# FFN down products as seven block products of 2x2 blocks, their sums into x by transfers and VectorE

## The chip, the cores and the metric

One core of a Trainium2 chip runs the kernel. The metric is the device time of one execution in microseconds. TensorE (PE) multiplies, VectorE (DVE) and ScalarE (ACT) do the elementwise work, GpSimd (POOL) and SyncE (SP) issue transfers.

## What is computed

Two layers of an encoder for 640 tokens (512 of a prompt, 8 x 16 of running streams), model width 1024. Each layer is a feed-forward half step, a mixer (convolution and attention branches) and a second feed-forward half step. All is fp32. The part that is changed is the feed-forward:

```python
def _swiglu(h, w_gu, w_down):
    gu = h @ w_gu
    g, u = jnp.split(gu, 2, axis=-1)
    return (jax.nn.silu(g) * u) @ w_down
...
    xp = xp + 0.5 * _swiglu(_rmsnorm(xp, norm_ffn1[l]), w_ffn1_gu[l], w_ffn1_down[l])
```

The inner width is 2816, so 22 inner tiles of 128 rows; the output has 8 tiles of 128.

## The kernel before

Activations lie transposed: `x[m]` is a tile of 128 channels x 640 tokens. fp32 products are made from fp32r parts: each weight and each activation is split into a high part (a ScalarE cast, `whi`, `ahi`) and a low part (a VectorE subtraction, `wlo`, `alo`), and a product is three matmuls: high x high, high x low (activation), low x high (weight). One matmul takes 128 x 128 weights and 320 tokens, half of the 640.

Weights come as a stream of 512 KB transfers (`raw`, three buffers, SP's queue). `prep` makes a slab of 8 weight tiles, 128x1024 (cast L264, low part L269), three buffers each. `slab`, `quiet`, `begin`, `ahead` and `flush` hand out slabs and place the preparation of later ones in the order.

The gate and up products (`gate_up`, a "gu" step, one for each inner tile j) are already made in seven products: the 2x2 block matrix [up; gate] x [even, odd input tiles] times [even, odd input tiles] x [first, second 320 tokens] takes seven block products instead of eight. Three of the seven use sums of weights, which `source` makes with four VectorE additions of 128x512 (L208) on each pair of `raw` tiles, so that 16 weight tiles give 3.5 slabs; `X11, X21, XN6, XT5, XT7, X22, XT4` name the seven forms of the input. A "gu" step is 7 blocks of 12 matmuls. Its accumulators `pa`, `pb`, `pc` are PSUM banks of the tag "att" (four), and ScalarE copies intermediate values of `pa` and `pc` out (`c1` L780, `u2` L791, `c5` L793), since `pa` goes on accumulating. Behind it stands its tail: silu, the product with `rho` (L811), with u (L812), and the split into `ahi` and `alo` (L181, L182).

The 22 inner tiles go in chunks, given by `FFNS`: a0 has (4, 2, 4, 4, 4, 4), b0 (2, 4, 4, 4, 8), a1 (2, 4, 4, 4, 4, 4), b1 (2, 4, 4, 4, 5, 3); a and b are the first and second feed-forward of layers 0 and 1. `ffn_order` puts the down products of one chunk between the gate/up steps of the next, two output tiles after each; those of the last chunk stand at the end. A down product (`product`, L337) of one output tile takes 4 inner tiles x 3 x 2 halves = 24 matmuls into one of two double banks (tag "acc": `pda`, `pdb`), and VectorE adds half of it to `x[m]` (L857, 128x640).

The order on PE, VectorE and ScalarE within a feed-forward is the order in which the program writes the instructions (`manual_schedule`); in the mixer a scheduler orders them. PE's next instruction waits for slabs, for tails and for accumulators that were copied out.

Of the kernel before, what the change touches and what calls it, by code (L numbers as in the profile page):

```python
# [16 lines left out]
P = 128  # L17
D = 1024
L = 2
# [27 lines left out]

PARTS = slice(0, 3 * P), slice(3 * P, T)

XT4, XN6, XT7, X21, X22, X11, XT5 = range(7)  # L50
UW = 2 + SEQ + NB * USEG

# [5 lines left out]
NSM = O_ST + L * CT * NB * 2  # L58


def ffn_order(name):

    chunks, plain = FFNS[name]
    out, held, j0 = [], [], 0
    for n in chunks:
        ms = list(range(KT)) if held else []
        step = max(2, -(-KT // n))
        for j in range(j0, j0 + n):
            out.append(("std" if j < plain else "gu", j))
            if ms:  # L70
                out.append(("down", [(m, held) for m in ms[:step]]))
                ms = ms[step:]
        held = list(range(j0, j0 + n))
        j0 += n

    return out + [("cut", None)] + [("down", [(m, held)]) for m in range(KT)]
# [18 lines left out]
def kinds():  # L95


    out = []

    def plain(n):  # L100
        out.extend([8] * (n // 8) + [n % 8] * (n % 8 > 0))

    def ffn(name):
        held = 0
        for what, a in ffn_order(name):
            if what == "gu":
                plain(held)
                held = 0
                out.append("gu")
            elif what == "std":  # L110
                held += 2 * KT
            elif what == "cut":
                plain(held)
                held = 0
            else:
                held += sum(len(js) for _, js in a)
        plain(held)

    for l in range(L):
        ffn(f"a{l}")  # L120
        held = 0
        for what, _ in mixer_order():
            if what == "mix":
                plain(held)
                held = 0
                out.append("mix")
            else:
                held += {"v": KT * AW // P, "o": KT}.get(what, CT)
        plain(held)
        ffn(f"b{l}")  # L130
    return out
# [11 lines left out]
def trunk(ctx: ExitStack, tc: tile.TileContext, xin, wst, small, pbias, samplebias, kcache, vcache,  # L143
# [36 lines left out]
    def split(hi, lo, src):  # L180
        ACT.copy(hi, src)  # L181
        DVE.tensor_tensor(out=lo, in0=src, in1=hi.bitcast(F32), op=ALU.subtract)  # L182
# [84 lines left out]
    def flush():  # L267
        for lo, src, hi in pending:
            DVE.tensor_tensor(out=lo, in0=src, in1=hi.bitcast(F32), op=ALU.subtract)  # L269
        pending.clear()  # L270
# [20 lines left out]
    def begin():  # L291

        prep(used[0] + 2)
# [30 lines left out]
    def soon():  # L324
        return tc.high_priority(offset=300)

    def steps(ps, ops, at=()):


        n = len(ops)  # L330
        for k, (xh, xl) in enumerate(ops):
            if k in at:
                at[k]()
            wh, wl = tiles.take()
            for j, (w, x) in enumerate(((wh, xh), (wh, xl), (wl, xh))):
                for a in range(2):
                    PE.matmul(ps[:, a, :HT], w, x[:, a * HT : (a + 1) * HT],  # L337
                              start=k == 0 and j == 0, stop=k == n - 1 and j == 2)
            yield

    def product(ps, ops, at=()):
# [362 lines left out]
        with soon():  # L704
            last(pa)

    def gate_up(fp, n, ex, first, turned, tails, put, j):

        pa, pb, pc = (att(f"p{i}{n}")[:, :HT] for i in "abc")

        def cap(name):
            return fp.tile([P, HT], F32, tag="cap", name=f"{name}{n}", bufs=4)

        def mul(ps, s, half, x, ks, start, stop):
            block(ps, s, half, lambda kp: tuple(z[:, x] for z in ex.ops[kp]), ks, start, stop)

        every, most, end = range(NP), range(NP - 1), range(NP - 1, NP)
        g, u = tmp(f"g{n}"), tmp(f"u{n}")
        t1, t2 = slice(0, HT), slice(HT, T)
        c1, u2, c5 = (cap(f"{i}_") for i in ("c1", "u2", "c5"))  # L720
        rho = ex.rho
        if first:

# [53 lines left out]
        else:  # L777
            s0 = quiet()
            mul(pa, s0, 0, X11, every, True, True)
            ACT.copy(c1, pa)  # L780
            prep(used[0] + 1)
            for t in tails:
                t()
            tails.clear()
            flush()
            mul(pb, s0, 1, X21, every, True, True)
            add(u[:, t1], pb, c1)
# [1 line left out]
            flush()  # L789
            mul(pa, s1, 0, XN6, every, False, True)  # L790
            ACT.copy(u2, pa)  # L791
            mul(pc, s1, 1, XT5, every, True, True)
            ACT.copy(c5, pc)  # L793
            s2 = slab(True)[0]
            mul(pa, s2, 0, XT7, every, False, True)
            add(g[:, t2], pa, c5)
            DVE.tensor_tensor(out=g[:, t2], in0=g[:, t2], in1=rho[:, t2], op=ALU.mult)
# [6 lines left out]
        mul(pa, s3, 0, XT4, every, False, True)  # L804
        DVE.tensor_tensor(out=g[:, t1], in0=pa, in1=rho[:, t1], op=ALU.mult)
        ACT.activation(g, g, AF.Silu, scale=-1.0)
        flush()

        def tail():
            begin()  # L810
            DVE.tensor_tensor(out=g, in0=g, in1=rho, op=ALU.mult)  # L811
            DVE.tensor_tensor(out=u, in0=u, in1=g, op=ALU.mult)  # L812
            flush()
            hi = hp.tile([P, T], F32R, tag="hhi", name=f"ahi{n}")
            lo = hp.tile([P, T], F32R, tag="hlo", name=f"alo{n}")
            split(hi, lo, u)
            put(j, (hi, lo))
            ahead()

        tails.append(tail)  # L820
        if first and turned:
            tails.append(ex.inverse)

    def ffn(name, fp, ex, goff, after, end=False):


        act, tails = {}, []
        nxt = None
        chunks, plain = FFNS[name]
        last = FT - chunks[-1]  # L830
        hold[0] = True
        if plain:
            ex = opening(fp, name, goff, plain, act.__setitem__, tails)
        for what, a in ffn_order(name):
            if what in ("std", "cut"):
                continue
            if what == "gu":
                turned = after is not None and not end
                gate_up(fp, f"{name}_{a}", ex, a == plain, turned, tails, act.__setitem__, a)
                continue  # L840
            js = a[0][1]
            if js[0] == last or len(a) * len(js) >= KT:
                for t in tails:
                    t()
                tails.clear()
            if after is not None and js[0] == last:
                nxt = nxt or after()
            if end and js[0] == last:
                nxt.all([act[j] for j in js])
                break  # L850
            for m, js in a:
                pd = acc(f"pd{name}_{js[0]}_{m}")
                product(pd, [act[j] for j in js])
                done = nxt and m == KT - 1
                if nxt:
                    nxt.weights(m)
                DVE.scalar_tensor_tensor(out=halves(x[m]), in0=two(pd), scalar=0.5,  # L857
                                         in1=halves(x[m]), op0=ALU.mult, op1=ALU.add)
                if not done:
                    flush()  # L860
                if nxt:
                    nxt.final(m)
        hold[0] = False
        if not nxt:
            flush()
        return nxt

    def mixer(l, after):
# [633 lines left out]
    for l in range(L):  # L1502
        if l == 0:
            open_pool("fp")
            ex = None
        with tc.manual_schedule(engines=ORDERED):
            ffn(f"a{l}", pool[0], ex, O_G1, None)
        fp.close()

        def after(st):  # L1510
            open_pool(f"fp{l}")
            return Expand(pool[0], f"b{l}", O_G2 + l * KT, st)

        ex = mixer(l, after)
        with tc.manual_schedule(engines=ORDERED):
            if l < L - 1:
                ex = ffn(f"b{l}", pool[0], ex, 0,
                         lambda: Expand(pool[0], f"a{l + 1}", O_G1 + (l + 1) * KT, ex))
            else:
                ffn(f"b{l}", pool[0], ex, 0, Final, True)  # L1520
    fp.close()
    ps.close()

# [7 lines left out]
def _stream(i):  # L1531
# [9 lines left out]
    for l in range(L):  # L1541
        def ffn(name, gu, down):
            g, u = _cols(gu[:, :FF]), _cols(gu[:, FF:])
            d = _cols(down)
            parts, held = [], []
            for what, a in ffn_order(name):
                if what == "gu":
                    if held:
                        parts.append(chunks(held))
                    held = []  # L1550

                    parts.append(chunks([z[a][o::2] for z in (u, g) for o in range(2)]))
                elif what == "std":
                    held += [g[a], u[a]]
                elif what == "cut":
                    parts.append(chunks(held))
                    held = []
                else:
                    held += [d[m][js[0] : js[-1] + 1] for m, js in a]
            return np.concatenate(parts + [chunks(held)])  # L1560
# [88 lines left out]
```

## Time and profile before

| | |
|---|---|
| median of 3 runs | 2574.33 us (2574.31 to 2575.58) |
| profiled execution | 2574.47 us |
| its span, first to last instruction | 2572.7 us |
| PE, VectorE, ScalarE, POOL busy | 99%, 75%, 44%, 2% |
| granted TensorE clock | 0.999 |
| matmuls | 17576 |
| weight stream | 384 transfers of 512 KB, 3.5 us to landing |

The profile's page gives the busy share of each engine, the chain of work that ended last, and groups of instructions by code line with the idle time in front of them. Views of the trace give the same by stretch (windows), in order of time (timeline) and by who waited for whom. `a` and `b` at the end of a tile's name stand for the two feed-forwards of a layer.

### The profile page before, as it was taken

The page shows a single profiled execution, that of the slowest core. Times are in us where ns is not written, and L with a number is a line of the kernel's source. Part 1 is how long each engine was busy: PE and PEld are TensorE (multiplying, and loading weights), DVE is VectorE, ACT ScalarE, POOL GpSimd, SP SyncE. Part 2 cuts the span into 40 slices and gives each one's busy share as a digit, 9 for nine tenths or more (in the row PEclk, how much of TensorE's full clock was granted, in tenths as well). Part 3 has the DMA queues.
Part 4 walks back from the last instruction along what each step waited for, and adds up shares of the span by engine and source line. Part 5 has one row for each costly group of instructions (what it writes and reads, how often), then busy time and mean ns, then how long its engine had stood idle before and what let it go on. Part 6 is the DMA issues. An engine that isn't in the chain of part 4 may idle for free.

```text
span 2572.7 us, 42534 instructions
## 1 busy us (share of the span) xinstructions
PE 2553.6 (99%) x17576; PEld 2497.1 (97%) x17576; DVE 1934.1 (75%) x2973; ACT 1144.7 (44%) x1802; POOL 60.5 (2%) x153
## 2 busy tenths in 40 slices
PE   8999999999999999999999999999999999999998
PEld 8999999888999999999999999998889999999998
DVE  7786767778777987677787767787786778777676
ACT  5343335575444543334444333356644445433333
POOL 0000000111000000000000000001110000000000
PEclk9999999999999999999999999999999999999999
DMA  3222223235222232222222222233442222222222
GB/s 133 66 100 91 81 75 108 99 116 168 75 83 88 74 102 74 81 89 78 83 82 99 74 90 83 74 101 113 134 136 83 74 91 81 92 83 74 91 91 74
DMA packets 74066, 237.05 MB, mean 92 GB/s; under 512 B 8241, under 2 KB 19121, under 8 KB 73873
## 3 DMA queue, kind: packets, MB, share of 16 engines
q1 hardware_dynamic: 70272, 223.90, 26.0%
q0 software_dynamic: 2880, 9.79, 1.1%
q8 instruction: 138, 2.26, 0.4%
q10 hardware_dynamic: 720, 0.65, 0.1%
q14 instruction: 56, 0.45, 0.1%
HBM read 225.85 MB, written 7.94 MB: 91 GB/s over the span
## 4 chain that ended last, share of the span: by engine, by line
PE 92%; DVE 4%; ACT 3%; issue 1%; DMA 0%; ACTq 0%; DVEq 0%
PE pab L351 12%; PE pda L337 12%; PE pdb L337 11%; PE paa L351 11%; PE pcb L351 6%; PE pca L351 5%; PE py L337 4%; PE po L337 4%; PE qa L351 4%; PE pbb L351 3%; PE pba L351 3%; PE pv L1160 2%; PE ma_cv L351 2%; PE ma_qk L351 2%; PE qc L351 2%; PE ma_b L351 1%
## 5 line engine op out<-in xcount | busy, mean ns | idle before, releaser
L269 DVE TENSOR_TENSOR wlo<-raw,whi 128x1024 fp32r<-128x1024 f32 (+2 forms) x540 | 562.5, 1047 | 189.5 <-ACT whi L264 187.3
L264 ACT CAST whi<-raw 128x1024 fp32r<-128x1024 f32 (+2 forms) x540 | 489.9, 912 | 253.7 <-PE pca L351 79.4
L351 PE MATMUL pab<-xhib,whi 128*128 128x320 f32 x704 | 218.4, 310 | 0.4 <-ACT u_b L791 0.4
L351 PE MATMUL pab<-xlob,whi 128*128 128x320 f32 x704 | 217.5, 309 | 0.0
L351 PE MATMUL pab<-xhib,wlo 128*128 128x320 f32 x704 | 217.5, 309 | 0.0
L351 PE MATMUL paa<-xhia,whi 128*128 128x320 f32 x640 | 198.2, 310 | 0.7 <-ACT c_a L727 0.5
L351 PE MATMUL paa<-xloa,whi 128*128 128x320 f32 x640 | 197.7, 309 | 0.0
L351 PE MATMUL paa<-xhia,wlo 128*128 128x320 f32 x640 | 197.7, 309 | 0.0
L337 PE MATMUL pda<-ahia,whi 128*128 128x320 f32 x704 | 160.3, 309 | 0.6 <-DVE x L857 0.6
L337 PE MATMUL pda<-ahia,wlo 128*128 128x320 f32 x704 | 160.4, 309 | 0.0
L337 PE MATMUL pda<-aloa,whi 128*128 128x320 f32 x704 | 160.4, 309 | 0.0
L264 ACT CAST whi<-s 128x1024 fp32r<-128x1024 f32 (+1 forms) x120 | 109.5, 912 | 111.8 <-DVE s L208 85.4
L337 PE MATMUL pdb<-ahib,wlo 128*128 128x320 f32 x656 | 149.5, 309 | 0.0
L337 PE MATMUL pdb<-alob,whi 128*128 128x320 f32 x656 | 149.4, 309 | 0.0
L337 PE MATMUL pdb<-ahib,whi 128*128 128x320 f32 x656 | 149.3, 309 | 0.0
L269 DVE TENSOR_TENSOR wlo<-s,whi 128x1024 fp32r<-128x1024 f32 (+1 forms) x120 | 127.2, 1060 | 13.1 <-ACT whi L264 13.1
L351 PEld LDWEIGHTS pab<-xhib,whi 128*128 128x128 f32 x704 | 132.2, 188 | 1.2 <-ACT u_b L791 0.9
L351 PEld LDWEIGHTS pab<-xlob,whi 128*128 128x128 f32 x704 | 132.2, 188 | 0.2
L351 PEld LDWEIGHTS pab<-xhib,wlo 128*128 128x128 f32 x704 | 132.1, 188 | 0.0
L351 PEld LDWEIGHTS paa<-xhia,whi 128*128 128x128 f32 x640 | 120.1, 188 | 1.3 <-ACT c_a L727 0.8
L351 PEld LDWEIGHTS paa<-xloa,whi 128*128 128x128 f32 x640 | 120.1, 188 | 0.1
L351 PEld LDWEIGHTS paa<-xhia,wlo 128*128 128x128 f32 x640 | 120.1, 188 | 0.0
(582 smaller groups left out, 6952.7 us busy)
## 6 DMA issues: line engine op xcount, KB each, us to landing
raw<-in_wst SPq DMA_DIRECT2D x384, 512.0 KB, 3.5
kc<-in_kcache SPq DMA_DIRECT2D x32, 256.0 KB, 4.0
vc<-in_vcache SPq DMA_DIRECT2D x16, 512.0 KB, 4.5
bias<-in_pbias POOLq DMA_DIRECT2D x16, 256.0 KB, 3.2
x<-in_xin SPq DMA_DIRECT2D x8, 320.0 KB, 5.1
out_vo<-v POOLq DMA_DIRECT2D x10, 256.0 KB, 2.5
out_ko<-k POOLq DMA_DIRECT2D x8, 320.0 KB, 2.5
out_yout<-x SPq DMA_DIRECT2D x8, 192.0 KB, 1.9
```

The lines of the kernel that those rows point to most:

```text
L264: ACT.copy(hi[:, d], src[:, c])
L269: DVE.tensor_tensor(out=lo, in0=src, in1=hi.bitcast(F32), op=ALU.subtract)
L337: PE.matmul(ps[:, a, :HT], w, x[:, a * HT : (a + 1) * HT], start=k == 0 and j == 0, stop=k == n - 1 and j == 2)
L351: PE.matmul(ps, a, b, start=start and kp == 0 and j == 0, stop=stop and kp == NP - 1 and j == 2, skip_group_check=True)
L1160: PE.matmul(pv[t], xx[:, t * P : (t + 1) * P], w[:, kk * AW : (kk + 1) * AW], start=c == 0 and kk == 0 and j == 0, stop=c == KT // 2 - 1 a ...
```

## The change

The down products of a chunk of four inner tiles that is neither the first plain one nor the last (`by_seven`) are made in the same seven-product form: 2x2 blocks of two output tiles by two inner tiles, times two inner tiles by two halves of the tokens. There are 13 such chunks: three in a0, b0 and b1, four in a1.

- A "rows" step (`down_rows`) makes four of the eight output tiles; two of them stand behind the second and the third gate/up step of the next chunk (`ROWS`). It takes 16 weight tiles, prepared as a "gu" slab group, and 7 x 12 = 84 matmuls. It uses both "acc" tiles (A, B) and two "att" banks (c).
- Each pair of inner tiles (`Pair`) gets its seven forms: the tail makes the halves and E1; `rest` makes XN6, XT4, XT7 with their high and low parts in five pieces, and `TURNS` says at which places of the later steps these pieces stand.
- The sums: B, c and the last state of A are added to x by VectorE (`take`, 128x320 each). Four intermediate states (c1, u2, c7 of A, c5 of c) are staged in SBUF by ScalarE with their factor and added to x by accumulating transfers that POOL issues (`send`, two of 128x320 each). The staging tiles are five of 128x2x320 (before: four of 128x320).
- From the third gate/up step of the first such chunk to the end of the gate/up steps only PE keeps the written order; VectorE and ScalarE are ordered by the scheduler.
- In a0 and a1, where the last chunk has four inner tiles, the first two of the final output tiles are multiplied together: for the first three inner tiles of both, then for the fourth of both.

```diff
+TURNS = (
+    ("r0d1", "g3e1", "g3e2", "g3e2", "g3e2"), ("g0e3", "g1e2", "g1e3", "g1e3", "g1e3"),
+    ("g2e3", "g2e4", "g2e7", "g2e7", "g2e7"), ("g0e3", "g0e4", "g0e7", "g0e7", "g0e7"),
+)
+ROWS = (1, 2)
...
-            if ms:
+            if ms and by_seven(name, held[0]):
+                if j - j0 in ROWS:
+                    out.append(("rows", (ms[:4], held)))
+                    ms = ms[4:]
+            elif ms:
...
+        def product(self, n, u, g, hi, lo):
+            if self.E is None:
+                z = self.E = self.fp.tile([P, 3, HT], F32, name=f"de{n}", tag="even", bufs=1)
+                DVE.tensor_tensor(out=z[:, 0:3:2], in0=halves(u), in1=halves(g), op=ALU.mult)
+                DVE.tensor_tensor(out=z[:, 1], in0=z[:, 0], in1=z[:, 2], op=ALU.subtract)
+                at, kinds = slice(0, 2), (X11, XT5)
+            else:
+                z = self.O = self.fp.tile([P, 5, HT], F32, name=f"do{n}", tag="odd", bufs=1)
+                DVE.tensor_tensor(out=z[:, 3:5], in0=halves(u), in1=halves(g), op=ALU.mult)
+                at, kinds = slice(3, 5), (X21, X22)
...
+            flush()
+            ACT.copy(halves(hi), z[:, at])
+            self.low(halves(lo), halves(hi), z[:, at])
...
+        def rest(self):
+            E, O = self.E, self.O
+            for o, a, b in ((XN6, E[:, 1], O[:, 4]), (XT4, O[:, XN6], O[:, 3])):
+                DVE.scalar_tensor_tensor(out=O[:, o], in0=a, scalar=-1.0, in1=b,
+                                         op0=ALU.mult, op1=ALU.subtract)
+            DVE.tensor_tensor(out=O[:, XT7], in0=O[:, 4], in1=E[:, 2], op=ALU.subtract)
+            yield
...
+    def down_rows(fp, n, ms, pairs, tails, later):
...
+        def stage(name, ps, scale=0.5):
+            z = fp.tile([P, 2, HT], F32, tag="cap", name=f"{name}{n}", bufs=5)
+            if ps is A:
+                ACT.activation(z, two(A), AF.Copy, scale=scale)
+            else:
+                for u in range(2):
+                    ACT.activation(z[:, u], ps[u], AF.Copy, scale=scale)
+            return z
+        def send(z, r, cols):
+            for u in range(2):
+                POOL.dma_start(x[ms[2 * u + r]][:, cols], z[:, u], accum_op=ALU.add)
+        def take(ps, r, cols, scale=0.5):
+            for u in range(2):
+                xs = x[ms[2 * u + r]][:, cols]
+                DVE.scalar_tensor_tensor(out=xs, in0=ps[u], scalar=scale, in1=xs, op0=ALU.mult, op1=ALU.add)
+        s0 = quiet()
+        mul(a, s0, 0, X11, True)
+        c1 = stage("c1_", A)
+        prep(used[0] + 1)
+        begin()
+        if not second:
+            tail()
+        flush()
+        place("d1")
+        mul(b, s0, 1, X21, True)
+        take(b, 0, t1)
+        send(c1, 0, t1)
+        s1 = slab(True)[0]
+        flush()
+        mul(a, s1, 0, XN6, False)
+        u2 = stage("u2_", A)
+        mul(c, s1, 1, XT5, True)
+        c5 = stage("c5_", c, -0.5)
+        s2 = slab(True)[0]
+        if second:
+            tail()
+        mul(a, s2, 0, XT7, False)
+        send(stage("c7_", A, -0.5), 1, t2)
+        send(c5, 1, t2)
+        flush()
+        ahead()
+        mul(c, s2, 1, X22, False)
+        take(c, 0, t2)
+        send(u2, 0, t2)
+        s3 = slab(True)[0]
+        ahead()
+        mul(a, s3, 0, XT4, False)
+        take(a, 1, t1, -0.5)
+        flush()
...
+            if what == "gu" and a == free:
+                order({mybir.EngineType.PE})
+            if what == "cut":
+                order(ORDERED)
...
+                    if m == 0:
+                        two_pd = [acc(f"pd{name}_{js[0]}_{i}") for i in range(2)]
+                        ws = [[tiles.take() for _ in js] for i in range(2)]
+                        for ks in (js[:-1], js[-1:]):
+                            for p, w in zip(two_pd, ws):
+                                for j in ks:
+                                    multiply(p, w[j - js[0]], act[j], j == js[0], j == js[-1])
```

More of the change, by code (lines that the diff above doesn't have):

```diff
@@ L58, with chunk_at, by_seven @@
 NSM = O_ST + L * CT * NB * 2
+def chunk_at(name, j):
+    at = 0
+    for n in FFNS[name][0]:
+        if j < at + n:
+            return at, n
+        at += n
+def by_seven(name, j):
+    at, n = chunk_at(name, j)
+    return n == 4 and at >= FFNS[name][1] and at + n < FT
 def ffn_order(name):
@@ L114, in ffn @@
                 held = 0
+            elif what == "rows":
+                plain(held)
+                held = 0
+                out.append("gu")
             else:
@@ L325, in soon, with multiply @@
         return tc.high_priority(offset=300)
+    def multiply(ps, ws, xs, first, last):
+        (wh, wl), (xh, xl) = ws, xs
+        for j, (w, x) in enumerate(((wh, xh), (wh, xl), (wl, xh))):
+            for a in range(2):
+                PE.matmul(ps[:, a, :HT], w, x[:, a * HT : (a + 1) * HT],
+                          start=first and j == 0, stop=last and j == 2)
     def steps(ps, ops, at=()):
@@ L333, in steps @@
                 at[k]()
[L334 to L338, printed above, removed]
+            multiply(ps, tiles.take(), (xh, xl), k == 0, k == n - 1)
             yield
@@ L705, in seven, with gate_up, spot @@
             last(pa)
-    def gate_up(fp, n, ex, first, turned, tails, put, j):
+    def gate_up(fp, n, ex, first, turned, tails, put, j, pair, later, at):
         pa, pb, pc = (att(f"p{i}{n}")[:, :HT] for i in "abc")
         def cap(name):
-            return fp.tile([P, HT], F32, tag="cap", name=f"{name}{n}", bufs=4)
+            return fp.tile([P, 2, HT], F32, tag="cap", name=f"{name}{n}", bufs=5)
         def mul(ps, s, half, x, ks, start, stop):
             block(ps, s, half, lambda kp: tuple(z[:, x] for z in ex.ops[kp]), ks, start, stop)
+        def spot(name):
+            step(later, f"g{at}{name}")
         every, most, end = range(NP), range(NP - 1), range(NP - 1, NP)
@@ L719, in gate_up @@
         t1, t2 = slice(0, HT), slice(HT, T)
-        c1, u2, c5 = (cap(f"{i}_") for i in ("c1", "u2", "c5"))
+        both = cap("c1_")
+        c1, u2, c5 = both[:, 0], both[:, 1], cap("c5_")[:, 0]
         rho = ex.rho
@@ L781, in gate_up @@
             prep(used[0] + 1)
+            spot("e1")
             for t in tails:
@@ L784, in gate_up @@
             tails.clear()
+            spot("e2")
             flush()
@@ L791, in gate_up @@
             ACT.copy(u2, pa)
+            spot("e3")
             mul(pc, s1, 1, XT5, every, True, True)
@@ L794, in gate_up @@
             s2 = slab(True)[0]
+            spot("e4")
             mul(pa, s2, 0, XT7, every, False, True)
@@ L806, in gate_up, with tail @@
         ACT.activation(g, g, AF.Silu, scale=-1.0)
+        spot("e7")
         flush()
-        def tail():
-            begin()
+        def tail(weights=True):
+            if weights:
+                begin()
             DVE.tensor_tensor(out=g, in0=g, in1=rho, op=ALU.mult)
-            DVE.tensor_tensor(out=u, in0=u, in1=g, op=ALU.mult)
-            flush()
             hi = hp.tile([P, T], F32R, tag="hhi", name=f"ahi{n}")
             lo = hp.tile([P, T], F32R, tag="hlo", name=f"alo{n}")
-            split(hi, lo, u)
+            if pair:
+                pair.product(n, u, g, hi, lo)
+            else:
+                DVE.tensor_tensor(out=u, in0=u, in1=g, op=ALU.mult)
+                flush()
+                split(hi, lo, u)
             put(j, (hi, lo))
-            ahead()
+            if weights:
+                ahead()
         tails.append(tail)
@@ L822, in gate_up, with __init__, low, keep @@
             tails.append(ex.inverse)
+    class Pair:
+        def __init__(self, fp, name, i, later, spots):
+            self.fp, self.name, self.i, self.later, self.spots = fp, name, i, later, spots
+            self.E, self.X, self.done = None, {}, 0
+        def product(self, n, u, g, hi, lo):
[8 more added lines that the diff above has]
+                at, kinds = slice(3, 5), (X21, X22)
+                self.later.append(self)
+                self.work = self.rest()
+            flush()
+            ACT.copy(halves(hi), z[:, at])
+            self.low(halves(lo), halves(hi), z[:, at])
+            self.keep(kinds, hi, lo)
+        def low(self, lo, hi, z):
+            DVE.tensor_tensor(out=lo, in0=z, in1=hi.bitcast(F32), op=ALU.subtract)
+        def keep(self, kinds, hi, lo):
+            for i, kind in enumerate(kinds):
+                c = slice(i * HT, (i + 1) * HT)
+                self.X[kind] = hi[:, c], lo[:, c]
+        def rest(self):
[5 more added lines that the diff above has]
+            yield
+            hi, lo = (hp.tile([P, T], F32R, tag=f"h{i}", name=f"t{i}{self.name}") for i in ("hi", "lo"))
+            ACT.copy(halves(hi), O[:, 1:3])
+            yield
+            self.low(halves(lo), halves(hi), O[:, 1:3])
+            self.keep((XN6, XT7), hi, lo)
+            yield
+            hi, lo = (self.fp.tile([P, HT], F32R, tag=f"t4{i}{self.i}", name=f"t4{i}{self.name}", bufs=1)
+                      for i in ("hi", "lo"))
+            ACT.copy(hi, O[:, 0])
+            yield
+            self.low(lo, hi, O[:, 0])
+            self.keep((XT4,), hi, lo)
+            yield
@@ new lines, in step, with mul, place, tail @@
+    def step(later, place):
+        for p in later:
+            while p.done < 5 and p.spots[p.done] == place:
+                next(p.work)
+                p.done += 1
+    def down_rows(fp, n, ms, pairs, tails, later):
+        A, B = (acc(f"d{i}{n}") for i in "ab")
+        a, b = ([z[:, u, :HT] for u in range(2)] for z in (A, B))
+        c = [att(f"dc{n}_{u}")[:, :HT] for u in range(2)]
+        t1, t2 = slice(0, HT), slice(HT, T)
+        second = ms[0] > 0
+        def mul(ps, s, half, kind, start):
+            for u in range(2):
+                for i, pair in enumerate(pairs):
+                    kp = half * NP + 2 * u + i
+                    wh, wl = (z[:, kp * P : (kp + 1) * P] for z in s)
+                    xh, xl = pair.X[kind]
+                    for j, (w, y) in enumerate(((wh, xh), (wh, xl), (wl, xh))):
+                        PE.matmul(ps[u], w, y, start=start and i == 0 and j == 0,
+                                  stop=i == 1 and j == 2, skip_group_check=True)
+        def place(name):
+            step(later, f"r{int(second)}{name}")
+        def tail():
+            for t in tails:
+                t(False)
+            tails.clear()
+        def stage(name, ps, scale=0.5):
+            z = fp.tile([P, 2, HT], F32, tag="cap", name=f"{name}{n}", bufs=5)
+            if ps is A:
+                ACT.activation(z, two(A), AF.Copy, scale=scale)
+            else:
+                for u in range(2):
[5 more added lines that the diff above has]
+        def take(ps, r, cols, scale=0.5):
+            for u in range(2):
+                xs = x[ms[2 * u + r]][:, cols]
[4 more added lines that the diff above has]
+        prep(used[0] + 1)
+        begin()
+        if not second:
[23 more added lines that the diff above has]
+        s3 = slab(True)[0]
+        ahead()
+        mul(a, s3, 0, XT4, False)
+        take(a, 1, t1, -0.5)
+        flush()
@@ L824, in ffn @@
     def ffn(name, fp, ex, goff, after, end=False):
-        act, tails = {}, []
+        act, tails, later, pairs = {}, [], [], {}
+        first_two = FFNS[name][0][-1] == 4
         nxt = None
@@ L831, in ffn, with order @@
         hold[0] = True
+        mode = ExitStack()
+        free = min(j for j in range(FT) if by_seven(name, j)) + 2
+        def order(engines):
+            mode.close()
+            mode.enter_context(tc.manual_schedule(engines=engines))
+        order(ORDERED)
         if plain:
@@ L834, in ffn @@
         for what, a in ffn_order(name):
+            if what == "gu" and a == free:
+                order({mybir.EngineType.PE})
+            if what == "cut":
+                order(ORDERED)
             if what in ("std", "cut"):
@@ L838, in ffn @@
                 turned = after is not None and not end
-                gate_up(fp, f"{name}_{a}", ex, a == plain, turned, tails, act.__setitem__, a)
+                pair = None
+                if by_seven(name, a):
+                    i, odd = divmod(a - chunk_at(name, a)[0], 2)
+                    if not odd:
+                        at = chunk_at(name, a)[0]
+                        rows = at and by_seven(name, at - 1)
+                        pairs[a] = Pair(fp, f"{name}_{a}", i, later, TURNS[i if rows else i + 2])
+                    pair = pairs[a - odd]
+                gate_up(fp, f"{name}_{a}", ex, a == plain, turned, tails, act.__setitem__, a, pair, later,
+                        a - chunk_at(name, a)[0])
+                continue
+            if what == "rows":
+                ms, js = a
+                down_rows(fp, f"{name}_{js[0]}_{ms[0]}", ms, [pairs[j] for j in js[::2]], tails, later)
                 continue
@@ L851, in ffn @@
             for m, js in a:
-                pd = acc(f"pd{name}_{js[0]}_{m}")
-                product(pd, [act[j] for j in js])
+                if js[0] == last and m < 2 and first_two:
+                    if m == 0:
[5 more added lines that the diff above has]
+                                    multiply(p, w[j - js[0]], act[j], j == js[0], j == js[-1])
+                    pd = two_pd[m]
+                else:
+                    pd = acc(f"pd{name}_{js[0]}_{m}")
+                    product(pd, [act[j] for j in js])
                 done = nxt and m == KT - 1
@@ L865, in ffn @@
             flush()
+        mode.close()
         return nxt
@@ L1505, in trunk @@
             ex = None
-        with tc.manual_schedule(engines=ORDERED):
-            ffn(f"a{l}", pool[0], ex, O_G1, None)
+        ffn(f"a{l}", pool[0], ex, O_G1, None)
         fp.close()
@@ L1514, in trunk @@
         ex = mixer(l, after)
[L1515 to L1520, printed above, removed]
+        if l < L - 1:
+            ex = ffn(f"b{l}", pool[0], ex, 0,
+                     lambda: Expand(pool[0], f"a{l + 1}", O_G1 + (l + 1) * KT, ex))
+        else:
+            ffn(f"b{l}", pool[0], ex, 0, Final, True)
     fp.close()
@@ L1557, in ffn @@
                     held = []
+                elif what == "rows":
+                    parts.append(chunks(held))
+                    held = []
+                    ms, js = a
+                    parts.append(chunks([d[m][js[0] + o : js[-1] + 1 : 2] for r in range(2)
+                                         for o in range(2) for m in ms[r::2]]))
                 else:
```

## The prediction

> **What bounds the kernel now.** I read the page first (shares of the engines, the chain that ended last), then TensorE's waits, then the chain in order of time around a place where gate/up steps follow each other, then windows and the timeline of VectorE there.
>
> ```profile
> span 2572.7 us, 42534 instructions
> PE 2553.6 (99%) x17576; PEld 2497.1 (97%) x17576; DVE 1934.1 (75%) x2973; ACT 1144.7 (44%) x1802; POOL 60.5 (2%) x153
> PE 92%; DVE 4%; ACT 3%; issue 1%; DMA 0%; ACTq 0%; DVEq 0%
> PE poa L337 <- ACT whi L584: 6.0, 1, 6.0
> ...
> PE paa L351 <- ACT u_a L791: 0.2, 1, 0.2
> 1232.40 56.31 PE pdb L337 x384
> 1197.20 1.76 PE pbb L351 x12
> ```
>
> TensorE is busy for 99% of the span and makes 92% of the chain. Its list of waits has eleven rows, from 6.0 us once at the start down to 0.2 us, and their sum is 13 us. So the time is the number of matmuls times their pitch. The chain gives the pitch: 56.31 us for 384 matmuls is 146.6 ns, in down products, and 1.76 us for 12 is the same 147 ns in gate/up blocks. (A row's 309 ns is one matmul from start to end; they overlap.)
>
> ```profile
> 1195.60:1207.90 12.30, 12.30 (x86) 12.30 (x86) 10.96 (x17) 6.00 (x9) 0.00 (x0) 1.00 0.25 87
> 1143.80:1182.70 38.90, 38.90 (x268) 38.90 (x267) 27.55 (x40) 14.51 (x20) 0.00 (x0) 1.00 0.26 82
> 1195.43 0.48 DVE L208 TENSOR_TENSOR ub<-pcb,u_b 128x320 f32<-128x320 f32 x1
> 1195.83 0.68 DVE L208 TENSOR_TENSOR raw<-raw,raw 128x512 f32<-128x512 f32 x1
> 1196.43 0.68 DVE L208 TENSOR_TENSOR raw<-s,raw 128x512 f32<-128x512 f32 x1
> 1197.04 0.48 DVE L805 TENSOR_TENSOR gb<-pab,rhob 128x320 f32<-128x320 f32 x1
> 1197.44 1.21 DVE L269 TENSOR_TENSOR wlo<-s,whi 128x1024 fp32r<-128x1024 f32 x1
> 1198.57 0.82 DVE L811 TENSOR_TENSOR gb<-gb,rhob 128x640 f32<-128x640 f32 x1
> 1199.42 0.82 DVE L812 TENSOR_TENSOR ub<-ub,gb 128x640 f32<-128x640 f32 x1
> 1200.16 1.82 DVE L269 TENSOR_TENSOR wlo<-raw,whi 128x1024 fp32r<-128x1024 f32 x2
> 1201.90 0.82 DVE L182 TENSOR_TENSOR alob<-ub,ahib 128x640 fp32r<-128x640 f32 x1
> 1202.63 0.48 DVE L208 TENSOR_TENSOR ub<-pbb,c_b 128x320 f32<-128x320 f32 x1
> 1204.35 0.49 DVE L208 TENSOR_TENSOR gb<-pab,c_b 128x320 f32<-128x320 f32 x1 [1.23 <-PE pab L351]
> 1206.42 0.68 DVE L208 TENSOR_TENSOR s<-raw 128x512 f32<-128x512 f32 x1
> 1207.14 0.69 DVE L208 TENSOR_TENSOR s<-s,raw 128x512 f32<-128x512 f32 x1
> 1182.68 1.55 DVE L857 SCALAR_TENSOR_TENSOR x<-pdb,x 128x640 f32<-128x640 f32 x2
> 1199.09 0.31 PE L351 MATMUL pab<-xhib,wlo 128*128 128x320 f32 x1
> ```
>
> The columns of a window are its length, then busy time of PE, weight load, DVE, ACT, POOL, then clock and DMA share. In the first one gate/up steps stand back to back: PE is full, VectorE has 10.96 us of work in 12.30 (89%). In the second (two gate/up steps, each with two down products) it has 71%. Start-to-start times give VectorE's pitch by width: 0.40 us for 320 elements, 0.60 for 512, 0.74 for 640 (0.85 where it needs the instruction before it), 1.13 for 1024. The timeline also shows how near the edge this already is: the low part of the slab of sums is done at 1197.44 + 1.21 = 1198.65, and the first matmul that reads it starts at 1199.09. That is 0.44 us of cover.
>
> **The change, part by part.**
>
> *Matmuls.* A chunk of four inner tiles costs 4 x 8 x 3 x 2 = 192 down matmuls; as seven products of half width it costs 7 x 2 pairs x 4 row pairs x 3 = 168. Thirteen chunks qualify (three each in a0, b0 and b1, four in a1), so 13 x 24 = 312 matmuls go. At 146.6 ns that is **45.7 us**, and all of it lies on the path, as PE waits for nothing there. Per chunk: 77.4 us (4 x 132 matmuls) become 73.9 (6 steps of 84).
>
> *VectorE.* Weight bytes stay the same, but the 16 weight tiles of each row step are now prepared as 3.5 slabs with four sums instead of two slabs. One row step: low parts 3 x 1.13 + 0.6 = 4.0, sums 0.72 + 3 x 0.61 = 2.5, six half-wide additions into x at 0.40 (the full one has a pitch of 1.55 - 0.82 = 0.73) = 2.4: 8.9 us. Each pair of inner tiles adds 0.40 (E1), three combinations (1.3 with their dependence) and low parts 0.74 + 0.40: 2.8. A chunk is then 4 x 10.96 + 2 x 8.9 + 2 x 2.8 = 67.2 us in 73.9, or 91%, where it was 55 in 77. It fits on average. In the order of the steps it is uneven, as the tails (0.85 + 0.74 + 0.73 = 2.3 us) and the combinations fall as `TURNS` puts them: gate/up 0 gets 12.3, gate/up 1 12.5, the first row step 12.6, against 12.3 of PE each; gate/up 2, the second row step and gate/up 3 get 8.6, 11.7 and 9.8. Three heavy steps in a row need 0.5 us more than PE takes, with 0.44 us of cover, and VectorE must still wait for PE in each (1.23 us above). So the bounds are 0 (the light steps before let it run ahead) and 3 x 1.23 - 0.44 + 0.5 = 3.7 us a chunk (none of its waits can be filled). The combinations of one pair are put right into that wait (`g0e3`), the low parts of the other pair too (`g1e3`), so I stay near the lower end: 0.7 us, 13 x 0.7 = **+9 us**; range 0 to +48.
>
> ```profile
> L780 ACT COPY c_b<-pab 128x320 f32<-128x320 f32 x42 | 17.7, 422 | 145.8 <-PE pab L351 145.8
> L264 ACT CAST whi<-raw 128x1024 fp32r<-128x1024 f32 x365 | 383.2, 1050 | 220.5 <-PE pca L351 79.4 <-PE pcb L351 69.4 <-PE qc L351 29.0
> L806 ACT ACTIVATE gb<-gb 128x640 f32<-128x640 f32 x44 | 32.6, 740 | 64.2 <-DVE gb L805 64.2
> ```
>
> *ScalarE.* Load is no issue: 6.0 of 12.3 us in a gate/up step; a row step has 3.8 of casts and 3.1 of staging. But PE comes back to the accumulator after 12 matmuls (1.76 us), and what must be copied out meanwhile has doubled: 0.74 instead of 0.42. Behind a cast of 1.05 that has just begun this makes 1.79, where it was 1.47. So a stage is late by nothing or by about 0.1 to 0.2 us; three of four can stall (after the last, c7, PE still has a block). I take one per row step, 26 x 0.1 = **+3 us**, bounds 0 and +16.
>
> *First and last steps of a feed-forward.* In a0 and a1 no down product stands behind the last gate/up step any more. The pair of products that is multiplied for three inner tiles first covers its tail with 36 x 0.147 = 5.3 us; the tail above ran from the end of XT4 (one block before the chain's 1197.20, so 1195.4) to 1202.7, 7.3 us, on a VectorE that was full. It is emptier there. Two places: 0 to +4, taken +1. The change of order (VectorE and ScalarE left to the scheduler after the first chunk) costs or saves nothing that a row shows; it moves the terms above within their bounds.
>
> *Transfers.* Each row step sends eight accumulating transfers of 160 KB on POOL's queue, which is idle in both windows.
>
> ```profile
> raw<-in_wst SPq DMA_DIRECT2D x384, 512.0 KB, 3.5
> out_ko<-k POOLq DMA_DIRECT2D x8, 320.0 KB, 2.5
> DMA to landing us min/median/max: 3.3/3.5/7.0
> 490.71 0.54 POOL L1134 DMA_DIRECT2D out_ko<-k  x1
> 1201.41 0.93 SPq L204 DMA_DIRECT2D raw<-in_wst  x2
> DMA packets 74066, 237.05 MB, mean 92 GB/s; under 512 B 8241, under 2 KB 19121, under 8 KB 73873
> q1 hardware_dynamic: 70272, 223.90, 26.0%
> 5.57 0.39 ACT L584 CAST whi<-raw 128x256 fp32r<-128x256 f32 x1
> 6.15 0.43 SPq L376 DMA_DIRECT2D raw<-in_wst  x1
> ```
>
> An issue is 0.54 us, a landing 2.5. c5 goes to the same half row as c7 and waits for its landing, and u2 is queued behind c5. c7 is staged after five blocks (8.8 us), so the last of the eight lands some 18 us after the step began, 6 us into the next one. The five staging buffers come round again only a whole gate/up step later, so nobody waits for this: cost nothing; the cover is that step of 12.3 us. What the transfers can do is slow the weights. The two of the window are issued at 1201.41 and 1202.0, land 3.5 later (1205.5), and the sum that needs them starts at 1206.42: 0.9 us of cover, then the 0.44. By the row of queue 1, 224 MB take 26.0% of 2572.7 us on 16 engines, so 1.31 MB take 3.9 us per row step beside the 3.1 that the window's share of 0.25 is: 57%. I take nothing for it.
>
> An accumulating transfer has no row here; if reading its target as well doubled its time, the 3.9 us would be 7.8 and the share 89%. The Trainium skill (Collectives: The Full Stack, the bandwidth ceiling) speaks for the doubled figure: there an add in the transfer is slow because it needs two source reads, which pushes twice the read traffic per byte. No run here shows it yet.
>
> **Sum.** 2574.47 us (the profiled execution; span 2572.7 and 1.8 around it) - 45.7 + 9 + 3 + 1 = 2541.8; the median shown is 2574.33, 0.14 less. Forecast **2541**, by itself 2533 to 2553.
>
> **Rivals.**
> - *All of it hidden.* VectorE runs ahead in the light steps, ScalarE's copies fit: 2574.3 - 45.7 = 2528.6, up to 2533. For it: 91% is hardly above the 89% at which PE shows no stall in the window. Against: the 0.44 us.
> - *VectorE becomes the bound of the three heavy steps.* 2 to 3.5 us a chunk, nearer the upper bound above: -45.7 + 13 x 2.5 = 2561 (2554 to 2574).
> - *The accumulating transfers hold up the weights*, the one that ends slower. The price counts from a landing of 3.5 + 0.9 + 0.44 = 4.84 us on; above it PE stalls by the rest, once per row step. It decides when the landing passes 4.84 + 45.7/26 = 6.6 us. At the longest landing in the trace (7.0) it is 26 x 2.16 = 56, that is 2585. For it: a share of 89%, if such a transfer takes twice the time; against: the eight are spread over 14 us and rarely two are under way together.
> - *The change doesn't do what it says*, since VectorE's addition to one half of a row waits for transfers into the other half. At the end of each row step this would be some 4 us, 26 x 4 = 104. Against it: the cast of the first columns of a tile ran at 5.57, before the last transfer into the same tile was issued at 6.15; waits go by the region. Next to no chance.
>
> **How the numbers follow.** Forecast 0.56, all hidden 0.20, VectorE bound 0.13, transfers 0.10, regions 0.01. 0.2% is 5 us, about what a measurement can tell here. Faster: 0.56 + 0.20 + 0.11 of the VectorE case = 0.87; same: 0.04 (that case's upper end, transfers at the point of decision); slower: 0.09. The range runs from the case with nothing lost, 2528, into the VectorE case, 2564, and leaves out its end and the transfers, 0.15 together.
>
> **What the changed profile would show.** 312 fewer matmuls; DVE up by 13 x 12 = 156 us to some 82% of the span; POOL with 208 issues. Right: PE's waits list wlo, whi and the stages with 10 to 15 us in sum. Wrong towards 2528: that list as short as now. Wrong upwards: wlo alone with over 25 us (VectorE), or sums that wait for raw transfers, with landings above 5 us.

## The result, and the profile after

| | before | changed |
|---|---|---|
| median of 4 runs | 2574.95 us | 2550.36 us (2548.09 to 2554.39) |
| ratio, 95% interval | | 0.9906 (0.9889 to 0.9923) |
| profiled execution | 2574.47 us | 2554.39 us |

The change makes the kernel faster by 24.6 us. The forecast was 2541, that is 33 us. 45.7 us of TensorE's work are gone; 21 of them came back as something else. The page after the change, in the order engines, queue of GpSimd's transfers, two of the costly groups (busy time, mean ns of one, then the idle time in front of them), landings of the transfers:

```profile
span 2552.6 us, 43143 instructions
PE 2517.7 (99%) x17264; PEld 2452.2 (96%) x17264; DVE 2095.1 (82%) x3337; ACT 1290.9 (51%) x2036; POOL 243.9 (10%) x361
q0 software_dynamic: 32832, 43.88, 10.1%
L240 DVE TENSOR_TENSOR s<-raw 128x512 f32<-128x512 f32 x110 | 75.7, 688 | 94.7 <-DMA raw<-in_wst 94.3
L975 POOL DMA_DIRECT2D x<-c_a x84 | 75.3, 961 | 799.7 <-ACT whi L296 589.6
raw<-in_wst SPq DMA_DIRECT2D x384, 512.0 KB, 3.6
x<-c_a POOLq DMA_DIRECT2D x84, 160.0 KB, 4.6
```

There are exactly 312 fewer matmuls, and VectorE has 161 us more to do. PE's rounded share of busy time is 99% as before, so the loss doesn't show there. What stands out is the idle time ahead of `s<-raw`, the sum of raw weight tiles: 94 us of waiting for weight transfers, where the list of VectorE's waits before had 1.5. An accumulating transfer takes 4.6 us from issue to landing in its largest group, and 0.96 us of GpSimd per issue there. The waits (us in total, times, longest), first those of PE's weight loads, PEld (the two longest rows), then VectorE's after and before the change:

```profile
PEld pab L386 <- DVE gb L240: 13.0, 17, 1.9
PEld paa L386 <- DVE ga L240: 11.6, 15, 1.5
```

```profile
DVE s L240 <- DMA raw<-in_wst: 94.3, 42, 4.4
```

```profile
DVE s L208 <- DMA raw<-in_wst: 1.5, 5, 0.4
```

13.0 + 11.6 = 24.6 us of PE: it waits for the addition `ga<-paa,c_a`, which reads XT7's value out of the accumulator before XT4 may go on in it. (The profiled execution is the longest of the four, 25.6 us above 2574.47 - 45.7; that the gain of the medians is also 24.6 us is chance.) 20 of these 32 waits, 18.8 us of them, come right behind a wait of VectorE for a weight transfer of 3.0 us or more; the other 12 come where it waited less or not at all. One such place in the chain of waits, in the gate/up step after a row step:

```profile
1509.44 1.15 DVE wlo L301
1510.59 0.02 issue
1510.60 5.24 DMA raw<-in_wst
...
1516.54 1.22 DVE wlo L301
1517.76 0.41 DVE ga L240
1518.17 0.04 issue
1518.21 3.79 PE paa L386 x24
```

VectorE's timeline there (start, length, instruction, and in brackets the idle time before it and what ended it):

```profile
1510.91 0.69 DVE L301 TENSOR_TENSOR wlo<-raw,whi 128x512 fp32r<-128x512 f32 x1
1515.93 0.69 DVE L240 TENSOR_TENSOR s<-raw 128x512 f32<-128x512 f32 x1 [4.33 <-DMA raw<-in_wst]
1516.54 1.22 DVE L301 TENSOR_TENSOR wlo<-raw,whi 128x1024 fp32r<-128x1024 f32 x1
1517.67 0.48 DVE L240 TENSOR_TENSOR ga<-paa,c_a 128x320 f32<-128x320 f32 x1
```

Windows of this step and the next, with columns as in the prediction; the last are granted clock, share of the DMA engines and GB/s:

```profile
1507.00:1519.50 12.50, 11.64 (x80) 11.38 (x79) 8.17 (x14) 4.30 (x7) 3.01 (x4) 1.00 0.71 150
1519.50:1532.00 12.50, 12.41 (x85) 12.15 (x84) 12.43 (x21) 6.99 (x11) 0.00 (x0) 1.00 0.26 85
```

A low part frees the raw buffer, the weight transfer is issued at 1510.60 and needs 5.24 us to land, while the DMA engines are 71% busy (26% in the next window): the row step's last accumulating transfers are under way. VectorE stands at `s<-raw` for 4.33 us. Behind it in VectorE's queue stand a low part and then `ga<-paa`; PE gets to XT4 about 1 us late. The sum itself isn't urgent: it is for the next step.

This seems to need two things together, late weights and a queue in which the sum stands ahead of the addition. Among the four VectorE instructions ahead of XT7's addition there is such a sum in 54 of 84 gate/up steps of the changed kernel, and in none before the change. So the theories for the experiments are: A, the accumulating transfers make the weights late; B, the order that the scheduler gave to VectorE turns that into a stall; and the rival C, VectorE at 91% is simply too full, frees the buffers late, and would stall without either.

### The profile page after: what moved, and what is told of

Its sections match the earlier page's. It is cut to its first block, busy times and chain, and to the rows that moved or that the text cites. A ratio compares the mean times of both kernels' runs of the same rounds, so it can differ in the third digit from the quotient of the medians.

```text
span 2552.6 us, 43143 instructions
## 1 busy us (share of the span) xinstructions
PE 2517.7 (99%) x17264; PEld 2452.2 (96%) x17264; DVE 2095.1 (82%) x3337; ACT 1290.9 (51%) x2036; POOL 243.9 (10%) x361
## 3 DMA queue, kind: packets, MB, share of 16 engines
q0 software_dynamic: 32832, 43.88, 10.1%
## 4 chain that ended last, share of the span: by engine, by line
PE 77%; DVE 13%; DMA 4%; ACT 3%; issue 2%; DVEq 0%; ACTq 0%
PE paa L386 10%; PE pab L386 8%; DVE wlo L301 5%; DMA raw<-in_wst 4%; PE py L363 4%; PE pdb L363 4%; PE po L363 4%; PE pda L363 4%; PE pca L386 4%; PE qa L386 4%; PE pcb L386 3%; PE daa L953 3%; PE pba L386 2%; PE pv L1392 2%; PE ma_cv L386 2%; PE dab L953 2%
## 5 line engine op out<-in xcount | busy, mean ns | idle before, releaser
L296 ACT CAST whi<-raw 128x1024 fp32r<-128x1024 f32 (+1 forms) x566 | 506.0, 898 | 390.7 <-PE pca L386 46.5
L301 DVE TENSOR_TENSOR wlo<-raw,whi 128x1024 fp32r<-128x1024 f32 (+1 forms) x566 | 581.5, 1031 | 120.3 <-ACT whi L296 116.6
L296 ACT CAST whi<-s 128x1024 fp32r<-128x1024 f32 (+1 forms) x146 | 137.9, 945 | 245.5 <-DVE s L240 107.6
L301 DVE TENSOR_TENSOR wlo<-s,whi 128x1024 fp32r<-128x1024 f32 (+1 forms) x146 | 158.8, 1088 | 13.8 <-ACT whi L296 13.8
L975 POOL DMA_DIRECT2D x<-c_b x72 | 65.4, 981 | 992.4 <-ACT whi L296 778.4
L240 DVE TENSOR_TENSOR s<-raw 128x512 f32<-128x512 f32 x110 | 75.7, 688 | 94.7 <-DMA raw<-in_wst 94.3
L975 POOL DMA_DIRECT2D x<-c_a x84 | 75.3, 961 | 799.7 <-ACT whi L296 589.6
L386 PEld LDWEIGHTS paa<-xhia,whi 128*128 128x128 f32 x640 | 120.0, 188 | 13.0 <-DVE ga L240 11.6
L386 PE MATMUL pcb<-xhib,whi 128*128 128x320 f32 x352 | 108.6, 309 | 0.0
L386 PE MATMUL pcb<-xlob,whi 128*128 128x320 f32 x352 | 108.6, 309 | 0.0
L386 PE MATMUL pcb<-xhib,wlo 128*128 128x320 f32 x352 | 108.6, 309 | 0.0
```

The lines of the kernel that those rows point to most:

```text
L240: DVE.tensor_tensor(out=out, in0=a, in1=b, op=ALU.add)
L296: ACT.copy(hi[:, d], src[:, c])
L386: PE.matmul(ps, a, b, start=start and kp == 0 and j == 0, stop=stop and kp == NP - 1 and j == 2, skip_group_check=True)
L975: POOL.dma_start(x[ms[2 * u + r]][:, cols], z[:, u], accum_op=ALU.add)
```

## Experiments

The first four ran on one chip beside before (2574.58 us), the others on another (2574.68 us). The first three keep the order of the instructions on VectorE, ScalarE and SP just as it is in the changed kernel.

**No transfers.**

```diff
-                POOL.dma_start(x[ms[2 * u + r]][:, cols], z[:, u], accum_op=ALU.add)
+                pass
```

> The four staged sums of each row step are not added to x (left out); all else, and the order on every engine, is as in the changed kernel. Theory A (accumulating transfers under way lengthen the landing of the weights from 3.5 to about 5.2 us, VectorE's queue stands at the sum s<-raw, and the addition of XT7 behind it comes late for PE's XT4): landings back to 3.5 us, VectorE's waits for raw transfers down from 94 us to under 45, the stalls of PE ahead of XT4 gone, 2529 to 2533 us. Theory C (VectorE is too full, so the raw buffers are freed late): nothing changes, 2548 to 2552 us.

Measured: 2530.31 us, ratio 0.9829 (0.9814 to 0.9844). VectorE's waits for raw transfers:

```profile
DVE s L240 <- DMA raw<-in_wst: 51.5, 38, 2.4
```

Of the waits of PE's weight loads ahead of XT4, 24.6 us in the changed kernel, one row is left:

```profile
PEld pab L386 <- DVE gb L240: 1.1, 2, 0.7
```

C falls: VectorE has the same work in the same order, and PE hardly waits. That VectorE's waits would drop below 45 us was a miss. They are still 51.5 us, at most 2.4 each instead of 4.4; waits of that length are covered.

**Plain copies.**

```diff
-                POOL.dma_start(x[ms[2 * u + r]][:, cols], z[:, u], accum_op=ALU.add)
+                POOL.dma_start(x[ms[2 * u + r]][:, cols], z[:, u])
```

> The transfers overwrite x instead of adding to it (the addition is left out): same bytes, same rows of 1280 bytes, same queue. If the addition itself (the second read) makes the transfers heavy: their landing falls from 4.4 to some 2.5 to 3 us, that of the weights to under 4.0, time 2533 to 2540 us. If it is the bytes or the short rows: landings as in the changed kernel, 2548 to 2552 us.

Measured: 2530.63 us, ratio 0.983 (0.9815 to 0.9845), below the 2533 to 2540 that was expected. Queue 0, and one of the groups of transfers:

```profile
q0 software_dynamic: 12864, 43.88, 4.8%
x<-c_a POOLq DMA_DIRECT2D x84, 160.0 KB, 2.2
```

The same 34 MB (43.88 less the 9.79 of before) take 4.8 - 1.1 = 3.7% of the 16 engines as copies and 10.1 - 1.1 = 9.0% as additions: 3.6 and 8.8 us per row step. It is the addition that is dear, by 2.4 times, and not the bytes or the short rows. It is also cut finer: (32832 - 2880)/208 = 144 packets a transfer, against 48. The prediction's estimate by the Trainium skill's rule on the two source reads (Collectives: The Full Stack, the bandwidth ceiling) was 7.8 us, by doubling; the trace agrees in direction, with somewhat more.

**Half of the transfers.**

```diff
-            for u in range(2):
+            for u in range(1):
                 POOL.dma_start(x[ms[2 * u + r]][:, cols], z[:, u], accum_op=ALU.add)
```

> Only the first of the two transfers of each send is made (half of the sums are left out). Theory A: the landing of the weights lies between, about 4.2 us in the row steps, and since 1.5 us or so of it is covered, more than half of the loss goes: 2533 to 2540 us. Theory C: 2548 to 2552 us.

Measured: 2530.80 us, ratio 0.983 (0.9815 to 0.9845).

```profile
DVE s L240 <- DMA raw<-in_wst: 49.3, 34, 2.7
x<-c_a POOLq DMA_DIRECT2D x42, 160.0 KB, 2.9
```

Not "more than half" of the loss is gone but all of it, and the weights don't land in between either. The first weight transfer issued behind each of the 26 row steps lands after 3.9 to 6.3 us in the changed kernel, 5.1 in the median; with half of the transfers the median is 3.3 us, as with plain copies and with none. Why half of them delay the weights by nothing no run shows. In the waits of VectorE there is a threshold: those of up to 2.7 us that are left in these three runs cost next to nothing, and of the 21 of 3.0 to 4.4 us in the changed kernel all but one make PE late.

**The sum behind the addition.** All transfers stay. The first sum of raw weights gets an ordering edge behind the last XT7 addition, without a wait:

```diff
-            add(g[:, t2], pa, c5)
+            seen[0] = add(g[:, t2], pa, c5)
...
-                    add(st[:, h2], rb[:, h1], rb[:, h2])
+                    behind(add(st[:, h2], rb[:, h1], rb[:, h2]))
...
+    def behind(i):
+        if seen[0] is not None:
+            tc.add_manual_dep(i.ins, seen[0].ins.name, mybir.DependencyInfo(
+                mybir.DependencyClass.NoSync, mybir.DependencyReason.DATA), reason="order")
+            seen[0] = None
```

> All transfers stay; only the order on VectorE is changed: the first sum of raw weights may not stand ahead of the addition of XT7 of the same gate/up step. Theory B (late weights cost only because the scheduler put their sum in front of the addition that PE waits for): landings stay at 5 us and more after row steps, the stalls ahead of XT4 go, 2531 to 2540 us. Theory A alone, with the order of no account: the sum is late for its own slab, PE waits for wlo instead, 2548 to 2555 us. Theory C: not faster than the changed kernel, 2550 us or more.

Measured: 2529.96 us (2529.23 to 2531.04), ratio 0.9827 (0.981 to 0.9843), 1 us below the range of theory B. VectorE's timeline at the same step:

```profile
1503.29 1.23 DVE L309 TENSOR_TENSOR wlo<-raw,whi 128x1024 fp32r<-128x1024 f32 x1 [3.18 <-ACT whi L304]
1504.43 0.48 DVE L242 TENSOR_TENSOR ga<-paa,c_a 128x320 f32<-128x320 f32 x1
1504.83 0.68 DVE L242 TENSOR_TENSOR s<-raw 128x512 f32<-128x512 f32 x1
```

Its waits for raw transfers, and the landings of the two weight transfers that were issued in this step:

```profile
DVE s L242 <- DMA raw<-in_wst: 7.5, 13, 1.3
```

```profile
DMA to landing us min/median/max: 5.3/5.4/5.6
```

The weights land late here too, after 5.4 us (4.9 in the median behind the 26 row steps), and hardly anything waits for them: the sum comes 0.4 us after the addition. VectorE is still idle for 3.18 us in this step, but ahead of a low part that waits for its cast, and the addition is in time. In the list of PE's weight loads one wait of 0.3 us for this addition is left. So A makes the lateness, B makes it cost. The edge did more than swap two instructions, though: the scheduler also moved others, some 560 of VectorE's 3337 in all and some 50 on ScalarE and GpSimd. That the sum's place is what counts rests on this run and the next together, which have different orders and in both of which the sum stands ahead of the addition in none of the 84 steps. This version does all of the computation and is the fastest here that does: 20 us below the changed kernel, 44.6 below before, where 45.7 is the worth of the matmuls.

**The written order everywhere.**

```diff
             if what == "gu" and a == free:
-                order({mybir.EngineType.PE})
+                order(ORDERED)
```

> VectorE and ScalarE keep the written order through all of the feed-forward, as before the change (the switch to the scheduler is undone); transfers stay. In the written order the sums of raw weights stand behind the addition of XT7. Theory B (a wait for late weights ahead of that addition is the whole loss): 2529 to 2536 us, with landings of 4.5 us and more after row steps. If the scheduler's order was needed to fit VectorE's 91%: 2540 us or more, with PE waiting for wlo or the stages.

Measured: 2545.93 us, ratio 0.9888 (0.9874 to 0.9903). Waits of PE, and of its weight loads:

```profile
PE pab L386 <- DVE wlo L301: 1.6, 2, 0.8
PE paa L386 <- DVE wlo L301: 1.6, 2, 0.8
```

```profile
PEld daa L953 <- ACT c_a L967: 3.3, 14, 0.2
PEld dab L953 <- ACT c_b L967: 3.2, 12, 0.6
```

VectorE's timeline at one of them:

```profile
200.63 0.81 DVE L902 TENSOR_TENSOR tloa<-doa,thia 128x640 fp32r<-128x640 f32 x1
201.86 0.49 DVE L902 TENSOR_TENSOR t4loa<-doa,t4hia 128x320 fp32r<-128x320 f32 x1 [0.42 <-ACT t4hia L924]
202.27 1.22 DVE L301 TENSOR_TENSOR wlo<-s,whi 128x1024 fp32r<-128x1024 f32 x1
```

The stall ahead of XT4 is gone, as B says, but the time is not: that this wait is the whole loss (2529 to 2536 us) was a miss, and the second reading held. Other stalls come: low parts of the pair stand in front of `wlo<-s`, and stages of the accumulator are late for PE. The scheduler's order has next to none of these and brought in the one bad place; it is 4.7 us worse than the written order as it stands and 16 us better with one edge added.

**Without the paired final products**, on the kernel with the edge.

```diff
-        first_two = FFNS[name][0][-1] == 4
+        first_two = False
```

> The kernel of e4_behind, with the first two final products of a0 and a1 one after the other again. If the tail of the last gate/up step is exposed without the pairing: two places of 3 to 5 us, 2536 to 2540 us. If VectorE and ScalarE are empty enough there: 2530 to 2532 us.

Measured: 2535.31 us, ratio 0.9848 (0.9834 to 0.9863), 5.3 us more than with the pairing, at two places:

```profile
PEld pda L371 <- ACT ahia L213: 3.5, 2, 1.8
PEld pda L371 <- DVE aloa L214: 1.6, 2, 0.8
```

PE waits for the high and then the low part of the last inner tile. The expected time for an exposed tail was 2536 to 2540; per place it is 2.7 us rather than 3 to 5.

**More work for VectorE**, on the kernel with the edge: each low part of the new inputs is computed twice.

```diff
             DVE.tensor_tensor(out=lo, in0=z, in1=hi.bitcast(F32), op=ALU.subtract)
+            DVE.tensor_tensor(out=lo, in0=z, in1=hi.bitcast(F32), op=ALU.subtract)
```

> The kernel of e4_behind, with each low part of the down products' inputs computed twice (the second gives the same values): 5.2 us more of VectorE per chunk, 72.4 in 73.9 us, or 98%. If VectorE's own load limits these steps (the term of +9 us of the prediction was of the right kind): PE waits for wlo and for additions, 1 to 3 us a chunk, 2543 to 2570 us. If only waits on transfers ever stalled it: 2530 to 2534 us.

Measured: 2548.36 us, ratio 0.9898 (0.9883 to 0.9913): 18.4 us or 1.4 a chunk.

```profile
PE paa L394 <- DVE wlo L309: 4.8, 5, 1.5
PE pab L394 <- DVE wlo L309: 4.3, 4, 1.6
```

The stall that the prediction reckoned with, `wlo` late for PE, exists; these rows hold half of the 18.4 us. By the reckoned load it sets in somewhere between 91% and 98% of VectorE in these steps, and the changed kernel is below it. (In the stretch from 230 to 378 us VectorE is busy for 89% with the edge alone and for 94% here.) The scheduler ordered this kernel anew as well, so how much of the loss is load and how much order is not shown.

**The changed kernel once more.**

> The changed kernel beside the others of this call: 2548 to 2554 us, with waits of VectorE for raw transfers of some 90 us again.

Measured: 2550.63 us, ratio 0.991 (0.9893 to 0.9926), as expected. PE's weight loads ahead of XT4, and VectorE's waits for raw transfers:

```profile
PEld pab L386 <- DVE gb L240: 11.3, 15, 1.9
PEld paa L386 <- DVE ga L240: 9.2, 15, 1.4
```

```profile
DVE s L240 <- DMA raw<-in_wst: 88.5, 36, 4.6
```

Here 20.5 us of PE's waits stand beside a loss of 22 against before less the matmuls (2574.68 - 45.7 = 2529.0).

## Why the prediction was right or wrong

The sign and the range were right; the likeliest time was 9 us too low, and the loss had another cause than the one that carried it. That the time fell into the range is partly luck: of the 13 us that were added for VectorE, ScalarE and the ends, nearly nothing came, and a term that was taken as nothing cost 21.

- *Matmuls.* Right: 312 fewer, at the pitch read from the chain. With the edge, 44.6 of the 45.7 us show.
- *VectorE, +9 us.* The load was right (161 us more, reckoned 156), the stall was not there: PE's list of waits has no row for `wlo`, and the first four experiments lose at most 2 us in all at the same load. The lower bound, nothing, held; whether by the light steps or by the waits that `TURNS` fills is not shown.
- *ScalarE, +3 us.* Weight loads wait 0.2 us for the row steps' stages under the scheduler and 6.5 us in the written order, for which the reckoning was made.
- *First and last steps, +1 us.* Nothing: with the pairing the list of waits has no row for these places that it didn't have before. The pairing is worth 5.3 us.
- *Transfers, taken as nothing.* This is the step that failed, in two ways. It took the engine time from plain transfers, 3.9 us a row step: as copies they do take 3.6, as additions 8.8. The landing was put at 2.5 us and is 4.6 in the largest group, the issue at 0.54 and is 0.96. And the 0.9 + 0.44 us of cover for the weights were read in the written order, where the sum follows the addition, while the step before had called the scheduler's order a matter that moves terms within their bounds. In the new order the wait for the weights stands ahead of what PE needs.
- *The third rival* had the first half of this mechanism, late weights, but with the sum's own slab as the way to PE. The profile's sign named for it, sums that wait for raw transfers and landings above 5 us, is what appeared. Its chance was put at 0.10, and its price was made in another way than the loss: PE loses what VectorE's wait exceeds some 2.5 to 3.2 us by, 0.5 to 1.8 us at 20 of the 26 row steps, and not what a landing exceeds 4.84 us by. By the rival's own rule the landings measured behind the row steps would have cost 10 us, not 21. They stayed below the 6.6 us from which it was to decide, which is why the time stayed inside the range.
- *Waits by region.* As read from the rows of the kernel's start: no addition to a half row waited for transfers into the other half (VectorE's list of waits names no `x` transfer).

## What to carry to other kernels

An off-path transfer isn't free when it shares engines with a load that an in-order queue waits for: ask which instruction stands behind that wait, and whether the critical engine needs it. When a busy share of 99% and a full VectorE hide the loss, the idle time ahead of one operation points at it (94 us against 1.5). It is no measure of the loss: some 50 us of the same waits cost next to nothing, and only the critical engine's own waits (24.6 us) give the price. Before taking a transfer or an operation back, try its order: one edge gave as much here as leaving the transfers out.

## What the runs showed of the hardware that was not expected

An accumulating transfer of 128 x 320 fp32 within SBUF costs 2.4 times the engine time of a copy of the same shape (9.0% against 3.7% of 16 engines for 34 MB), three times the packets (144 against 48), twice the landing (4.6 us against 2.2), and more of GpSimd per issue (0.96 us, where the plain copies took 0.54); landing and issue are those of the largest group. Behind the row steps, the first weight transfer of 512 KB landed after 5.1 us in the median (3.9 to 6.3) beside all of them, and after 3.3 us beside half of them, beside plain copies, or with none.
